# Up-projection of a gated MLP by seven block products instead of eight, with the gated tiles kept in DRAM

## The chip, the cores and the metric

One NeuronCore of a Trainium2 chip runs the whole kernel. The metric is the device time of one execution in microseconds. The engines are called PE (TensorE), DVE (VectorE), ACT (ScalarE), POOL (GpSimd) and SP (SyncE, which issues the DMAs here).

## The reference, cut to what matters

The model is one layer with a mixer sub-layer and a channel sub-layer on 1024 tokens of 1024 channels, all in float32. The change concerns the channel sub-layer:

```python
FFN_DIM = 2816
def conv_ffn(h, w_up, conv_w, conv_b, w_down, rows, cols):
    u, v = jnp.split(h @ w_up, 2, axis=-1)            # (1024, 1024) @ (1024, 2 * 2816)
    u = dwconv2d(u, conv_w, conv_b, rows, cols)       # 3x3, depthwise, on a 16 x 64 grid of tokens
    return (jax.nn.gelu(u) * v) @ w_down
...
        x = x + mx[2] * ox                            # first residual, after w_out of the mixer
        hx2 = modulate(rmsnorm(x, norm_ffn_w[l]), mx[3], mx[4])
        x = x + mx[5] * conv_ffn(hx2, ffn_w_up[l], ffn_conv_w[l], ffn_conv_b[l], ffn_w_down[l], rows, GRID_W)
    return rmsnorm(x, final_norm_w)
```

## The kernel before

Activations lie with channels on the 128 partitions and tokens along the free dimension (T = 1024 tokens, H = 512 in a half). Every matrix product works on float32 numbers split into two parts, `hi` and `lo`, and sums three terms: hi x hi, hi x lo, lo x hi. `gdense` (L117) issues them: for each k tile of 128 input channels three matmuls of 128x128 weights on 512 tokens, for each half. Each matmul has its own weight load. `wload` (L77) loads a tile of weights (128 x 1024, 512 KB) into `raw` and splits it: ACT copies `hi`, DVE subtracts for `lo` (`split`, L164). It does so with high priority, into two rooms used in turn.

The order of the work on each engine is made ahead of the run by the framework's scheduler, from the order of the program, from what is ready by its own estimate, and from priority. On the chip every engine then runs its list in order and waits on semaphores. Generators are interleaved by `weave` (L137): so many steps of a side job for each step of the main one.

`tail` (L1219) holds the channel sub-layer. `wout` (L1112) makes the mixer's output product in two halves of the tokens, with the first residual and the sums of squares for the second norm. `norm` (L1097) sums them over partitions with small matmuls, takes 1/rms, spreads it over the partitions, and its `apply` makes the modulated activations, split into `fh` and `fl` (8 k tiles each, the tiles A0 to A15). The norm of the first half runs beside `wout` of the second half, the norm of the second half beside the first `up`.

`up` (L1127) is run for f = 0 to 21. Tile f of u (weights f) goes into `pu`, a two-bank PSUM tile with tag `d` of which there are two; the convolution runs from there on DVE, eight steps of one tap each after ACT's Identity for the middle tap. Tile f of v (weights 22 + f) goes into two one-bank tiles with tag `s` (four of them). Gelu on ACT, the gating with v on DVE, and the split into `h` and `l` follow, which stay in SBUF (tiles H0 to H15). After f = 6 and f = 13 a round of `down` (L1175) multiplies the seven finished tiles by their part of the down-projection, adding into the residual x1; the last eight tiles are taken by `last_down` (L1191), in three pieces of the tokens, with the final norm beside it. Of the weights of the last round, the first are loaded early into the A tiles, which are free by then.

## Time and profile before

| | us |
|---|---|
| median of 3 runs | 2357.77 (2351.71 to 2358.16) |
| span of the profiled execution | 2358.4 |
| PE busy | 2301.8 (98%) |
| DVE busy | 1617.5 (69%) |
| ACT busy | 1067.5 (45%) |
| POOL busy | 3.4 |

The span runs from the first to the last instruction of one profiled execution. Busy times overlap between engines. The channel sub-layer takes the last 740 us of the span, from 1618.5 us, where `wout` ends, on.

### The profile page before, as it was taken

What the parts mean: (1) busy time and instruction counts of PE and PEld (TensorE: products, weight loads), DVE (VectorE), ACT (ScalarE), POOL (GpSimd) and SP (SyncE); (2) the same over time, 40 slices, a digit from 0 to 9 for tenths busy, and PEclk for the clock granted to TensorE, in tenths of its full rate; (3) what the DMA queues carried; (4) which work ended last, traced back from release to release, by engine and by line L of the source; (5) the groups of instructions that cost most, each with busy time, mean ns of one, the idle gap of its engine ahead of it and who ended that gap; (6) DMA issues with size and microseconds to landing.
All of it is one profiled execution on the core that took longest, in us unless ns stands there. A gap on an engine that the chain in (4) does not pass through costs nothing.

```text
span 2358.4 us, 29544 instructions
## 1 busy us (share of the span) xinstructions
PE 2301.8 (98%) x11530; PEld 1926.7 (82%) x11530; DVE 1617.5 (69%) x2618; ACT 1067.5 (45%) x1633; POOL 3.4 (0%) x16
## 2 busy tenths in 40 slices
PE   7999999999999999999999999999999999999998
PEld 3778878778888888888888878888888888888888
DVE  4877877889978858668876675557765267436655
ACT  4477667677766546646635232333221122112221
POOL 0000000000000000000000000000000000000000
PEclk8999999999999999999999999999999999999999
DMA  6212222144435333423428675532111111111112
GB/s 249 98 60 81 86 83 70 59 128 148 131 100 160 114 119 110 150 83 133 148 92 272 224 240 186 165 100 72 45 53 42 54 49 44 47 53 54 45 54 72
DMA packets 81455, 251.79 MB, mean 107 GB/s; under 512 B 9730, under 2 KB 15906, under 8 KB 76068
## 3 DMA queue, kind: packets, MB, share of 16 engines
q1 hardware_dynamic: 81312, 249.90, 32.5%
q8 instruction: 91, 1.49, 0.3%
q14 instruction: 48, 0.39, 0.1%
q10 hardware_dynamic: 4, 0.01, 0.0%
HBM read 222.33 MB, written 27.54 MB: 106 GB/s over the span
## 4 chain that ended last, share of the span: by engine, by line
PE 78%; DVE 11%; DMA 5%; ACT 4%; issue 2%; DVEq 0%; SPq 0%; ACTq 0%
PE d L124 37%; PE s L124 28%; PE s L982 2%; PE s L990 2%; DMA adar<-in_ada 2%; ACT L L162 2%; PE s L656 2%; DVE wlo L159 1%; DMA gk<-gd 1%; DVE L L159 1%; PE s L931 1%; PE s L932 1%; PE s L314 1%; DVE L L156 1%; DMA raw<-in_w 1%
## 5 line engine op out<-in xcount | busy, mean ns | idle before, releaser
L124 PE MATMUL d<-H,whi 128*128 128x512 f32 x2464 | 690.4, 398 | 1.2 <-ACT whi L162 1.0
L124 PEld LDWEIGHTS d<-H,whi 128*128 128x128 f32 x2464 | 450.6, 188 | 88.7 <-ACT whi L162 1.9
L162 ACT ACTIVATE whi<-raw 128x1024 fp32r<-128x1024 f32 (+1 forms) x194 | 203.2, 1049 | 581.5 <-PE s L124 347.5
L124 PE MATMUL d<-H,wlo 128*128 128x512 f32 x1232 | 385.9, 392 | 0.4 <-DVE wlo L159 0.3
L159 DVE TENSOR_TENSOR wlo<-raw,whi 128x1024 fp32r<-128x1024 f32 (+1 forms) x194 | 234.2, 1209 | 204.3 <-ACT whi L162 201.4
L124 PEld LDWEIGHTS d<-H,wlo 128*128 128x128 f32 x1232 | 230.2, 188 | 49.2 <-DVE wlo L159 1.7
L124 PE MATMUL s<-A,whi 128*128 128x512 f32 x960 | 258.4, 389 | 0.0
L124 PE MATMUL d<-A,whi 128*128 128x512 f32 x960 | 258.3, 389 | 0.0
L124 PE MATMUL s<-H,whi 128*128 128x512 f32 x832 | 251.3, 390 | 0.2 <-ACT whi L162 0.2
L156 DVE SCALAR_TENSOR_TENSOR facc<-d,vec,facc 128x945 f32<-128x945 f32 (+5 forms) x184 | 216.7, 1178 | 11.2 <-ACT facc L162 5.9
L124 PEld LDWEIGHTS d<-A,whi 128*128 128x128 f32 x960 | 180.1, 188 | 37.6
L124 PEld LDWEIGHTS s<-A,whi 128*128 128x128 f32 x960 | 180.2, 188 | 37.3
L124 PEld LDWEIGHTS s<-H,whi 128*128 128x128 f32 x832 | 155.9, 188 | 33.2 <-ACT whi L162 0.7
L162 ACT ACT_TABLE_LOAD x107 | 137.3, 1283 | 76.3 <-DVE cacc L156 28.7
L124 PE MATMUL s<-H,wlo 128*128 128x512 f32 x416 | 157.1, 390 | 2.8 <-DVE wlo L159 2.8
L156 DVE SCALAR_TENSOR_TENSOR M<-s,mods,M 128x512 f32<-128x512 f32 (+1 forms) x72 | 49.6, 690 | 160.7 <-PE s L124 160.5
L124 PE MATMUL d<-A,wlo 128*128 128x512 f32 x480 | 149.2, 389 | 0.2 <-DVE wlo L159 0.2
L124 PE MATMUL s<-A,wlo 128*128 128x512 f32 x480 | 149.1, 389 | 0.0
L124 PEld LDWEIGHTS d<-A,wlo 128*128 128x128 f32 x480 | 90.0, 188 | 19.2 <-DVE wlo L159 0.6
L124 PEld LDWEIGHTS s<-A,wlo 128*128 128x128 f32 x480 | 90.1, 188 | 18.7
L162 ACT ACTIVATE m<-GU,dtt 128x128 f32<-128x128 f32 x256 | 78.9, 389 | 48.5 <-PE s L982 43.5
L156 DVE SCALAR_TENSOR_TENSOR m<-GL,dtt,m 128x128 f32<-128x128 f32 x256 | 77.0, 345 | 29.5 <-ACT m L162 29.0
(274 smaller groups left out, 3191.4 us busy)
## 6 DMA issues: line engine op xcount, KB each, us to landing
raw<-in_w SPq DMA_DIRECT2D x92, 512.0 KB, 3.6
E<-csd SPq DMA_DIRECT2D x32, 1024.0 KB, 4.9
raw<-in_wup SPq DMA_DIRECT2D x44, 512.0 KB, 3.4
R<-csd SPq DMA_DIRECT2D x64, 256.0 KB, 3.9
adar<-in_ada SPq DMA_DIRECT2D x32, 512.0 KB, 4.3
gated<-sg SPq DMA_DIRECT2D x32, 256.0 KB, 2.5
gd<-y SPq DMA_DIRECT2D x32, 256.0 KB, 4.4
gk<-gd SPq DMA_DIRECT2D x32, 256.0 KB, 3.7
```

Source lines behind the costliest of these rows:

```text
L124: nc.tensor.matmul(o, a[:, k, :], b[k][:, xo + s : xo + e], start=(k == 0 and i == 0), stop=(k == kn - 1 and i == 2))
L156: self.nc.vector.scalar_tensor_tensor(out, in0, s, in1, op0=op0, op1=op1)
L159: self.nc.vector.tensor_tensor(out, a, b, op=op)
L162: self.nc.scalar.activation(out, in_, f, **kw)
L314: self.nc.tensor.matmul(ps[:2, :], scc[:, k, :], w[:, k, :], start=(k == 0), stop=(k == 7))
L656: nc.tensor.matmul(pg, a[:, q, :], b[:, s:e], start=(i == 0), stop=(i == 2))
L931: nc.tensor.matmul(ps[:, s - s2, 0, :], btok[:, s, :], xw[:, 0, s, :], start=True, stop=True)
L932: nc.tensor.matmul(ps[:, s - s2, 1, :], btok[:, 7 - s, :], xw[:, 1, 7 - s, :], start=True, stop=True)
L982: nc.tensor.matmul(psy[:, c, :], self.xt[:, c0 + c, h, :], m[:, h, c, :], start=(h == 0), stop=(h == 1))
L990: nc.tensor.matmul(pso[:, c, :], S[:, cc if d == 0 else 7 - cc, d, :], CT[:, cc * P : (cc + 1) * P], start=True, stop=True)
```

## The change

For each f the up-projection is seen as a product of 2 x 2 blocks: two tiles of outputs (u and v) by two halves of the 1024 input channels, times two halves of the channels by two halves of the tokens. Eight block products become seven (`PRODUCTS`), a form of Strassen's with sums of weights (`up_sums`, `up_split`) and sums of activations (`blocks` in `tail`). A block product has 4 k tiles x 3 terms on 512 tokens. Sums and `lo` parts of the weights are made on POOL (`ptt`). Blocks of activations are made once, in `blocks`, for all f. Partial products are collected in PSUM and in three SBUF tiles (`up_product`). Convolution, Gelu and gating of tile f (`up_post`) run beside the products of f + 1. The gated tile is stored to DRAM (`h_d`); `hload` brings it back and splits it for `down`. All 22 `up` come first, then both rounds of `down`, then the last. Two masks of the SSD stage (`mU`, `mL`, two affine_select on POOL) move from `setup` to `ssd`. Comments and docstrings go. Of the diff the part on the channel sub-layer, with deleted lines left out where they are printed above:

```diff
@@ -1124,53 +1124,154 @@
     ROUNDS = [(0, 7), (7, 14), (14, 22)]
-    def up(self, f, x, split, parts):
...
+    PRODUCTS = ("11", "12", "s2", "s1", "s3", "s4", "22")
+    def ptt(self, out, a, b, op):
+        self.nc.gpsimd.tensor_tensor(out, a, b, op=op)
+    def up_load(self, f, x):
+        raw = []
+        for i in range(2):
+            r = self.t(x["pA"], T, f"A{12 + 2 * (f % 2) + i}")
+            self.nc.sync.dma_start(r, self.A["wup"][f + NF * i])
+            raw.append(r)
+        x["raw"][f] = raw
+    def up_sums(self, f, x):
+        u, v = x["raw"][f]
+        q = self.t(self.wp, T, "raw")
+        a, b = q[:, :H], q[:, H:]
+        self.ptt(a, v[:, :H], v[:, H:], ALU.add)
+        self.ptt(b, a, u[:, :H], ALU.subtract)
+        x["sums"][f] = (a, b)
+    def up_split(self, f, p, x):
+        u, v = x["raw"][f]
+        a, b = x["sums"].get(f, (None, None))
+        src = {"11": u[:, :H], "12": u[:, H:], "22": v[:, H:], "s1": a, "s2": b, "s3": a, "s4": b}[p]
+        self.pslot = (self.pslot + 1) % 4
+        w = self.t(self.wp, T, ("whi0", "wlo0", "whi1", "wlo1")[self.pslot], F32R)
+        hi, lo = w[:, :H], w[:, H:]
+        self.act(hi, src, AF.Copy)
+        self.ptt(lo, src, hi.bitcast(F32), ALU.subtract)
+        if p == "s1":
+            self.ptt(a, u[:, :H], v[:, :H], ALU.subtract)
+        elif p == "s2":
+            self.ptt(b, u[:, H:], b, ALU.subtract)
+        x["w"][f, p] = [q.rearrange("p (k m) -> p k m", k=4) for q in (hi, lo)]
+    def up_product(self, f, p, x):
+        st = x["st"].setdefault(f, {})
+        if p == "11":
+            st["u"] = self.t(self.psD, T, "d")
+        elif p == "s3":
+            st["z"] = self.t(self.psS, H, "s")
+        ps = st["z"] if p in ("s3", "22") else st["u"][:, :H] if p == "12" else st["u"][:, H:]
+        hi, lo = x["w"].pop((f, p))
+        for k in range(4):
+            while x["b"][p][k] is None:
+                next(x["blocks"])
+            bh, bl = x["b"][p][k]
+            for i, (a, b) in enumerate(((hi, bh), (hi, bl), (lo, bh))):
+                self.nc.tensor.matmul(ps, a[:, k, :], b, start=(k == 0 and i == 0 and p in ("11", "12", "s3")),
+                                      stop=(k == 3 and i == 2), skip_group_check=True)
+            yield
+        if p == "11":
+            st["s1"] = self.t(self.p1, H, "sql")
+            self.act(st["s1"], ps, AF.Copy)
+        elif p == "12":
+            self.tt(ps, ps, st["s1"], op=ALU.add)
+        elif p == "s2":
+            st["s2"] = self.t(self.p2, H, "ssq")
+            self.act(st["s2"], ps, AF.Copy)
+        elif p == "s1":
+            st["s4"] = self.t(self.p1, H, "s4") if f % 2 else self.t(self.gp, H, "sg")
+            self.act(st["s4"], ps, AF.Copy)
+        elif p == "s3":
+            self.tt(st["s4"], ps, st["s4"], op=ALU.add)
+        elif p == "22":
+            self.tt(st["s2"], ps, st["s2"], op=ALU.add)
+    def up_post(self, f, x):
+        st = x["st"][f]
+        yield
+        acc = self.t(self.p2, T, "facc")
         wc = [self.v("ffn_conv_w", tap * NF + f) for tap in range(9)]
         a3 = acc.rearrange("p (r c) -> p r c", c=64)
...
+        u3 = st["u"].rearrange("p (r c) -> p r c", c=64)
+        self.act(acc, st["u"], AF.Identity, bias=self.v("ffn_conv_b", f), scale=wc[4])
+        for n, tap in enumerate((1, 7, 0, 2, 3, 5, 6, 8)):
+            dy, dx = tap // 3 - 1, tap % 3 - 1
+            r0, r1 = max(0, -dy), 16 - max(0, dy)
+            c0, c1 = max(0, -dx), 64 - max(0, dx)
+            o = a3[:, r0:r1, c0:c1]
+            self.stt(o, u3[:, r0 + dy : r1 + dy, c0 + dx : c1 + dx], wc[tap], o)
+            if n % 2:
+                yield
+        self.act(acc, acc, AF.Gelu_apprx_tanh)
+        yield
+        for i, v in ((1, st["s4"]), (0, st["s2"])):
+            self.tt(acc[:, i * H : i * H + H], acc[:, i * H : i * H + H], v)
+        self.st.dma_start(self.h_d[f], acc)
+        del x["st"][f]
+        yield
+    def ups(self, x):
+        first = [(0, "11"), (1, "11"), (0, "12"), (1, "12"), (0, "s2"), (1, "s2"), (0, "s1"), (1, "s1"), (0, "s4"),
+                 (0, "s3"), (1, "s3"), (1, "s4"), (0, "22")]
+        seq = list(first)
+        for f in range(2, NF):
+            seq += [(f, "11"), (f - 1, "22")] + [(f, p) for p in ("s2", "12", "s1", "s3", "s4")]
+        seq.append((NF - 1, "22"))
+        self.pslot = 0
+        side = []
+        for f in range(2):
+            self.up_load(f, x)
+            self.up_sums(f, x)
+        for q in seq[:2]:
+            self.up_split(*q, x)
+        for i, (f, p) in enumerate(seq):
+            if i + 2 < len(seq):
+                g, q = seq[i + 2]
+                self.up_split(g, q, x)
+                if q == "22" and g + 2 < NF:
+                    self.up_load(g + 2, x)
+            yield from self.up_product(f, p, x)
+            if (f, p) == (1, "s4") or (p == "12" and 1 < f < NF - 1):
+                self.up_sums(f + 1, x)
+            for g in list(side):
+                if next(g, "end") == "end":
+                    side.remove(g)
+            if p == "s4":
+                g = self.up_post(f, x)
+                next(g)
+                side.append(g)
+            if f == NF - 1:
+                for g in {"12": (0, 1), "s1": (2, 3), "s3": (4,), "s4": (5,), "22": (6,)}.get(p, ()):
+                    self.hload(g, x, self.t(x["pA"], T, f"A{12 + g % 4}"))
+        x["side"] = side
+    H_ROOM = (("A0", "A1"), ("A2", "A3"), ("H4", "H5"), ("H6", "H7"), ("A4", "A5"), ("A6", "A7"), ("H0", "H1"),
+              ("H2", "H3"), ("H8", "H9"), ("H10", "H11"), ("H12", "H13"), ("H14", "H15"), ("A8", "A9"), ("A10", "A11"),
+              ("A0", "A1"), ("A2", "A3"), ("H4", "H5"), ("H6", "H7"), ("A4", "A5"), ("A6", "A7"), ("H0", "H1"),
+              ("A14", "A15"))
+    WD_ROOM = (("H2", "H3"), ("H8", "H9"), ("H10", "H11"), ("H12", "H13"), ("H14", "H15"), ("A8", "A9"),
+               ("A10", "A11"), ("A12", "A13"))
+    def room(self, x, tag, dt=F32R):
+        return self.t(x["pA"] if tag[0] == "A" else self.pH, T, tag, dt)
+    def hload(self, f, x, raw=None):
+        raw = self.t(self.p2, T, "facc") if raw is None else raw
+        self.nc.sync.dma_start(raw, self.h_d[f])
+        h, l = [self.room(x, q) for q in self.H_ROOM[f]]
+        self.split(raw, h, l)
         x["h"][f] = (h, l)
...
     def down(self, r, x):
         a, b = self.ROUNDS[r]
@@ -1178,6 +1279,11 @@
         xh, xl = [x["h"][f][0] for f in range(a, b)], [x["h"][f][1] for f in range(a, b)]
         for m in range(8):
             w = self.wload(self.A[f"wd{r}"][m], kn * P, kn)
+            for g in list(x["side"]):
+                if next(g, "end") == "end":
+                    x["side"].remove(g)
+            if a + kn + m < self.ROUNDS[r + 1][1]:
+                self.hload(a + kn + m, x)
             for hf in range(2):
                 s, e = hf * H, hf * H + H
                 ps = self.t(self.psS, H, "s")
@@ -1201,8 +1307,7 @@
             while len(x["wd"]) < min(m + 3, 8):
                 q = len(x["wd"])
                 with (self.prio() if q < 2 else nullcontext()):
-                    hi = self.t(pA, T, f"A{2 * q}", F32R)
-                    lo = self.t(pA, T, f"A{2 * q + 1}", F32R)
+                    hi, lo = [self.room(x, n) for n in self.WD_ROOM[q]]
                     raw = self.t(self.wp, T, "raw")
                     nc.sync.dma_start(raw, self.A[f"wd{r}"][q])
                     self.split(raw, hi, lo)
@@ -1217,22 +1322,83 @@
     WAIT = (5, 3)
     def tail(self, mh, ml, pA, pM, out):
...
         nc, tc = self.nc, self.tc
         with tc.tile_pool(name="t1", bufs=1) as self.p1, tc.tile_pool(name="t2", bufs=2) as self.p2:
             x1 = [self.t(pM, T, f"M{k}") for k in range(8)]
...
+            self.h_d = self.dram([NF, P, T], "hd")
+            x = {"x1": x1, "h": {}, "wd": [], "pA": pA, "raw": {}, "sums": {}, "w": {}, "st": {}}
             sums = {}
...
-            def second(hf):
...
+            halves = lambda q: (q[:, :H], q[:, H:])
+            first = [halves(self.t(pA, T, f"A{k}", F32R)) for k in range(8)]
+            x["b"] = {p: [None] * 4 for p in self.PRODUCTS}
+            x["b"]["11"], x["b"]["12"] = first[:4], first[4:]
+            b8, b9 = [self.t(pA, T, f"A{k}") for k in (8, 9)]
+            b11 = [b8[:, :H], b8[:, H:], b9[:, :H], self.t(self.p1, H, "s4")]
+            def shifted(k, s, e, rs, t):
+                self.stt(t, x1[k][:, s:e], self.sc2[:, k : k + 1], rs, op0=ALU.mult, op1=ALU.mult)
+                return self.mods[:, 24 + k : 25 + k]
+            def apply0(k, rs):
+                t = self.t(self.p2, T, "facc")[:, :H]
+                xh, xl = first[k]
+                shift = shifted(k, 0, H, rs, t)
+                self.act(xh, t, AF.Identity, bias=shift)
+                if k < 4:
+                    self.act(b11[k], t, AF.Identity, bias=shift)
+                self.stt(xl, t, shift, xh.bitcast(F32), op0=ALU.add, op1=ALU.subtract)
+            def blocks():
+                for _ in range(3):
+                    yield
+                r = self.token_rs(self.p1, sums[1], H, 1.0 / D, "fr")
+                for _ in range(3):
+                    yield
+                rs = self.t(self.psS, H, "s")
+                self.spread(self.p2, r, rs, "fr")
+                yield
+                def split(p, k, src, tag):
+                    q = halves(self.room(x, tag))
+                    self.act(q[0], src, AF.Copy)
+                    self.tt(q[1], src, q[0].bitcast(F32), op=ALU.subtract)
+                    x["b"][p][k] = q
+                    return q
+                both, t2 = [], []
+                for k in range(4):
+                    q = halves(self.t(self.pH, T, f"H{12 + k}"))
+                    both.append(q)
+                    for i in range(2):
+                        shift = shifted(k + 4 * i, H, T, rs, q[i])
+                        self.act(q[i], q[i], AF.Identity, bias=shift)
+                    a, b = halves(self.t(self.p2, T, "facc"))
+                    self.tt(a, q[1], q[0], op=ALU.subtract)
+                    self.tt(b, a, b11[k], op=ALU.add)
+                    t2.append(split("s2", k, b, f"H{4 + k}"))
+                    yield
+                for k in range(4):
+                    a, _ = halves(self.t(self.p2, T, "facc"))
+                    self.ptt(a, both[k][0], b11[k], ALU.subtract)
+                    split("s1", k, a, f"H{k}")
+                    yield
+                for k in range(4):
+                    split("s4", k, both[k][1], f"A{(10, 11, 8, 9)[k]}")
+                    yield
+                for k in range(4):
+                    a, _ = halves(self.t(self.p2, T, "facc"))
+                    self.tt(a, both[k][1], both[k][0], op=ALU.subtract)
+                    split("s3", k, a, f"H{8 + k}")
+                    yield
+                for k in range(4):
+                    a, _ = halves(self.t(self.p2, T, "facc"))
+                    b21 = first[4 + k]
+                    self.tt(a, b21[0].bitcast(F32), t2[k][0].bitcast(F32), op=ALU.subtract)
+                    self.tt(a, a, b21[1].bitcast(F32), op=ALU.add)
+                    self.tt(a, a, t2[k][1].bitcast(F32), op=ALU.subtract)
+                    split("22", k, a, f"H{12 + k}")
+                    yield
             def final(i):
                 s, e = self.PIECES[i]
@@ -1245,16 +1411,13 @@
             for m in range(8):
                 nc.sync.dma_start(x1[m], self.A["xT"][m])
+            self.weave(self.wout(mh, ml, x1, 0, sums), None, 1)
+            self.weave(self.wout(mh, ml, x1, 1, sums), self.norm(sums[0], H, apply0, (5, 3)), self.RATIO[4])
+            x["blocks"] = blocks()
+            self.weave(self.ups(x), x["blocks"], self.RATIO[4])
+            for r in range(len(self.ROUNDS) - 1):
+                self.down(r, x)
             side = None
...
-            ends = {b: r for r, (a, b) in enumerate(self.ROUNDS[:-1])}
...
-                self.weave(self.up(f, x, f == 0, 2 if f == NF - 1 else 1), side, self.RATIO[4])
...
-                    self.down(ends[f], x)
             for i in range(len(self.PIECES)):
                 self.weave(self.last_down(i, x, sums), side, self.RATIO[5])
                 side = final(i)
```

## Rows read from the trace of the kernel before

**Rows 1.** The page: span, and busy time, share and instructions of each engine.
```profile
span 2358.4 us, 29544 instructions
PE 2301.8 (98%) x11530; PEld 1926.7 (82%) x11530; DVE 1617.5 (69%) x2618; ACT 1067.5 (45%) x1633; POOL 3.4 (0%) x16
```
**Rows 2.** The chain that ended last, in time: start us, us, what (L124 is `gdense`).
```profile
1618.48 4.08 PE d L124 x18
...
1643.24 10.88 PE d L124 x48
...
1784.68 87.04 PE s L124 x384
...
2241.64 56.55 PE s L124 x258
```
**Rows 3.** Waits of PE, 1520 to 2358 us: total us, times, longest.
```profile
PE d L208 <- DVE frdg L207: 1.9, 1, 1.9
PE d L198 <- DVE sql L159: 0.9, 1, 0.9
```
**Rows 4.** Stretches: us; busy (count) PE PEld DVE ACT POOL; granted PEclk; DMA, GB/s.
```profile
1665.00:1686.76 21.76, 21.76 (x97) 18.02 (x97) 17.95 (x17) 5.34 (x6) 0.00 (x0) 1.00 0.16 48
1784.68:1860.84 76.16, 76.16 (x337) 63.06 (x337) 30.60 (x32) 10.45 (x11) 0.00 (x0) 1.00 0.16 50
```
**Rows 5.** Groups by shape, 1618 to 2300 us: busy us, mean ns, idle before.
```profile
L156 DVE SCALAR_TENSOR_TENSOR facc<-d,vec,facc 128x945 f32<-128x945 f32 x84 | 101.0, 1202 | 2.9
L159 DVE TENSOR_TENSOR wlo<-raw,whi 128x1024 fp32r<-128x1024 f32 x43 | 52.5, 1221 | 103.4 <-ACT whi L162 102.9
L159 DVE TENSOR_TENSOR facc<-facc,s 128x512 f32<-128x512 f32 x44 | 28.3, 684 | 4.0 <-ACT facc L162 3.1
L162 ACT ACTIVATE facc<-d,vec 128x1024 f32<-128x1024 f32 x21 | 25.0, 1192 | 0.0
L162 ACT ACTIVATE facc<-facc 128x1024 f32<-128x1024 f32 x21 | 22.3, 1064 | 13.0 <-DVE facc L156 13.0
L162 ACT ACTIVATE sg<-M 128x512 f32<-128x512 f32 x6 | 3.8, 630 | 21.4 <-DVE M L156 21.4
L162 ACT ACTIVATE facc<-d,vec 128x512 f32<-128x512 f32 x2 | 1.5, 770 | 6.3 <-PE d L124 6.3
```
**Rows 6.** Groups of POOL by shape, the whole run.
```profile
L707 POOL MEMSET xt<- 128x512 f32 x2 | 1.0, 532 | 349.3 <-PE d L124 349.3
...
L282 POOL TENSOR_SCALAR_AFFINE_SELECT mU<-ones 128x128 f32<-128x128 f32 x1 | 0.3, 292 | 0.0
...
L240 POOL MEMSET btok<- 64x4 f32 x1 | 0.1, 100 | 0.1
```
**Rows 7.** DMA issues: count, KB each, median us from issue to landing.
```profile
raw<-in_wup SPq DMA_DIRECT2D x44, 512.0 KB, 3.4
...
M<-ad SPq DMA_DIRECT2D x8, 512.0 KB, 6.0
```
**Rows 8.** Second norm, second half, PE and DVE: start us, us, what [idle before].
```profile
1622.40 0.28 PE L198 MATMUL d<-ones,ssq 128*128 128x1 f32 x2
...
1627.79 1.41 DVE L156 SCALAR_TENSOR_TENSOR facc<-M,sc,d 128x512 f32<-128x512 f32 x2 [0.58 <-PE d L208]
1629.33 1.41 DVE L156 SCALAR_TENSOR_TENSOR A<-facc,mods,A 128x512 fp32r<-128x512 f32 x2
1630.66 1.40 DVE L156 SCALAR_TENSOR_TENSOR facc<-M,sc,d 128x512 f32<-128x512 f32 x2
```
**Rows 9.** Stretches at the start of the run (columns as in rows 4).
```profile
20.00:25.00 5.00, 0.98 (x4) 0.92 (x4) 3.77 (x8) 3.60 (x5) 0.00 (x0) 0.57 1.01 414
25.00:30.00 5.00, 0.80 (x4) 0.83 (x4) 4.83 (x9) 2.81 (x3) 0.00 (x0) 0.50 0.67 274
...
35.00:40.00 5.00, 4.03 (x17) 3.57 (x18) 2.45 (x11) 0.84 (x2) 0.00 (x0) 0.50 0.00 0
40.00:45.00 5.00, 5.00 (x23) 2.09 (x22) 1.57 (x4) 2.62 (x4) 0.00 (x0) 0.88 0.25 84
```

More of the change, by code (lines that the diff above doesn't have):

```diff
@@ L276, in setup @@
         self.ones = self.t(cpool, P, "ones")
-        self.mU = self.t(cpool, P, "mU")
-        self.mL = self.t(cpool, P, "mL")
         nc.gpsimd.memset(self.ones, 1.0)
@@ L702, in ssd @@
             self.bc, self.grp, self.pair, self.E, self.yst = {}, {}, {}, {}, {}
+            self.mU = self.t(q1, P, "mU")
+            self.mL = self.t(q1, P, "mL")
+            nc.gpsimd.affine_select(out=self.mU, in_=self.ones, pattern=[[1, P]], compare_op=ALU.is_ge,
+                                    fill=0.0, base=0, channel_multiplier=-1)
+            nc.gpsimd.affine_select(out=self.mL, in_=self.ones, pattern=[[-1, P]], compare_op=ALU.is_ge,
+                                    fill=0.0, base=0, channel_multiplier=1)
             dtt, cst, wtt = [self.t(q1, [NC, 16, 4], n) for n in ("dtt", "cst", "wtt")]
@@ L1125 @@
     ROUNDS = [(0, 7), (7, 14), (14, 22)]
-    def up(self, f, x, split, parts):
-        A, p2, fh, fl = self.A, self.p2, x["fh"], x["fl"]
-        pu = self.t(self.psD, T, "d")
-        spans = [[(0, H)], [(H, T)]] if split else [self.FULL]
-        wu = self.wload(A["wup"][f])
-        if split:
-            wv = self.wload(A["wup"][NF + f])
-            pv = [self.t(self.psS, H, "s") for _ in range(2)]
-            for sp in spans[:1]:
-                yield from self.gdense(pu, wu, fh, fl, sp)
-                yield from self.gdense(pv, wv, fh, fl, sp)
-            spans = spans[1:]
-        for sp in spans:
-            yield from self.gdense(pu, wu, fh, fl, sp)
-        acc = self.t(p2, T, "facc")
+    PRODUCTS = ("11", "12", "s2", "s1", "s3", "s4", "22")
@@ L1142, in up @@
+    def up_post(self, f, x):
+        st = x["st"][f]
+        yield
+        acc = self.t(self.p2, T, "facc")
         wc = [self.v("ffn_conv_w", tap * NF + f) for tap in range(9)]
         a3 = acc.rearrange("p (r c) -> p r c", c=64)
-        u3 = pu.rearrange("p (r c) -> p r c", c=64)
-        step = 16 // parts
-        for q in range(parts):
-            lo, hi = q * step, q * step + step
-            self.act(a3[:, lo:hi], u3[:, lo:hi], AF.Identity, bias=self.v("ffn_conv_b", f), scale=wc[4])
-            for tap in (1, 7, 0, 2, 3, 5, 6, 8):
-                dy, dx = tap // 3 - 1, tap % 3 - 1
-                r0, r1 = max(lo, -dy), min(hi, 16 - max(0, dy))
-                c0, c1 = max(0, -dx), 64 - max(0, dx)
-                o = a3[:, r0:r1, c0:c1]
-                self.stt(o, u3[:, r0 + dy : r1 + dy, c0 + dx : c1 + dx], wc[tap], o)
@@ L1155, in up @@
-        if not split:
-            wv = self.wload(A["wup"][NF + f])
-            pv = [self.t(self.psS, H, "s") for _ in range(2)]
-        for sp in spans:
-            yield from self.gdense(pv, wv, fh, fl, sp)
-        i = f % 8
-        h = self.t(self.pH, T, f"H{2 * i}", F32R)
-        l = self.t(self.pH, T, f"H{2 * i + 1}", F32R)
-        step = T // parts
-        for q in range(parts):
-            sl = slice(q * step, q * step + step)
-            self.act(acc[:, sl], acc[:, sl], AF.Gelu_apprx_tanh)
-            for i in range(2 * q // parts, 2 * (q + 1) // parts):
-                hs = slice(i * H, i * H + H)
-                self.tt(acc[:, hs], acc[:, hs], pv[i])
-            self.act(h[:, sl], acc[:, sl], AF.Copy)
-            self.tt(l[:, sl], acc[:, sl], h[:, sl].bitcast(F32), op=ALU.subtract)
+        u3 = st["u"].rearrange("p (r c) -> p r c", c=64)
@@ L1247, in tail @@
                 nc.sync.dma_start(x1[m], self.A["xT"][m])
-            side = None
-            for hf in range(2):
-                self.weave(self.wout(mh, ml, x1, hf, sums), side, self.RATIO[4])
-                side = second(hf)
-            ends = {b: r for r, (a, b) in enumerate(self.ROUNDS[:-1])}
-            for f in range(NF):
-                self.weave(self.up(f, x, f == 0, 2 if f == NF - 1 else 1), side, self.RATIO[4])
-                side = None
-                if f in ends:
-                    self.down(ends[f], x)
+            self.weave(self.wout(mh, ml, x1, 0, sums), None, 1)
[4 more added lines that the diff above has]
+                self.down(r, x)
+            side = None
             for i in range(len(self.PIECES)):
```

13 lines of the change are left out of this document (removed).

## The prediction, made before the change was run

> **What bounds the kernel now.** I read the page first: TensorE (PE) is busy 98% of the 2358.4 us span, VectorE (DVE) 69%, ScalarE (ACT) 45%, GpSimd (POOL) nothing [rows 1]. A share is a mean over stages, so next comes the chain that ended last, for the stretch from the end of w_out (1618.5 us) on. It is PE line 124 throughout: 48 matmuls in 10.88 us for each half of an `up`, and 384 in 87.04 us for the last half `up` before a round together with that round [rows 2]. Both are 0.2267 us a matmul, so PE runs without a gap. The waits of PE from 1520 us to the end confirm it: two, 2.8 us together, both in the second norm [rows 3]. One `up` in steady state takes 21.76 us, PE busy for all of it at full clock, DVE 17.95, ACT 5.34, POOL 0 [rows 4]. So a matmul removed here is worth 0.2267 us, as long as the other engines keep up, and PE never waits for new data.
>
> **Part 1, the products.** An `up` has 2 tiles x 8 k x 3 terms x 2 halves = 96 matmuls. Seven products of 4 k x 3 terms on 512 tokens are 84, of the same shape. Seen as time: 96 x 0.2267 = 21.76 us (as the row says) becomes 19.04 us; 22 times the 2.72 us saved is **59.8 us**. The two rounds of `down` and the last one keep their matmuls.
>
> **Part 2, what each tile asks of the other engines in 19.04 us.** DVE: eight taps at about 1.20 us (9.6), three half-wide additions of products at 0.68 (2.0), two gatings at 0.68 (1.4): 13.0 us, less than now, since the splits of weights and of h leave it [rows 5]. ACT: seven half-wide copies at 0.63 (4.4), three evictions of PSUM at 0.77 (2.3), one Identity of 1.19 and one Gelu of 1.06: 9.0 us [rows 5]. Both fit. POOL is new: seven `lo` subtractions and four sums a tile, 11 operations of 128x512 with two inputs. No row shows one. From below: a memset of 128x512, which reads nothing, 0.53 us. An affine_select of 128x128, one input, takes 0.29; less the 0.10 of a memset of four columns, that is 1.5 ns a column [rows 6]. A second input doubles this at most: 0.10 + 512 x 3.0 ns = 1.64 us. I take 1.21 (memset's 0.84 ns a column plus 0.66 ns for each input), nearest to the affine_select, which reads. Then 11 take 13.3 us, between 5.8 and 18.0: inside 19.04 even at the upper end. So in steady state I charge nothing; the cover is POOL's spare 5.7 us a tile, and if POOL took over 1.73 us an operation, PE would follow POOL. A gain is excluded, as PE has no wait there now.
>
> The Trainium skill (GPSIMD Engine Reference, Performance versus the Vector engine) gives 4497 ns for a tensor_tensor of 2048 columns; a quarter of it, an estimate of 1.12 us an operation, would make 12.4 us a tile and the same sum. No run here shows it yet.
>
> Three new waits of PE lie in each tile: products 11, s2 and s1 add into the same half of the `d` tile, and each is copied out by ACT before the next adds to it. One other product of 2.72 us stands between each pair; a copy needs 0.77 [rows 5]. One Gelu or Identity ahead of it on ACT still fits (1.19 + 0.77), two and a wait do not: see rival B. The store of h waits on SP for the gating; behind it stand only the loads of the tile after next, some 15 us early at 3.4 us each [rows 7]: nothing.
>
> **Part 3, the head (where I expect the loss).** Let 0 be the end of w_out, 1618.5 us in the old trace. Only products 11 and 12 of tiles 0 and 1 can run on the first half of the tokens: 4 x 2.72 = 10.9 us. All else needs blocks of the second half. Today the sums for the norm are issued at 1622.40 and the first scaling starts at 1627.79, 5.4 us later; with the change they are issued after three steps (2.0 us), so scaling starts at about 7.4 [rows 8]. From there DVE must do, half-wide: 20 operations for the s2 blocks (two scalings, two sums, one `lo` for each k), 4 for s1, 4 for s4, 8 for s3, 16 for 22, and four additions of products: 56 at the 0.66 us at which such operations follow each other [rows 8], 37.0 us, and 0.6 for one unhidden ACT step: until 45. The taps of tile 0 come after them in the program, 9.6 us: until **54.6**. Tile 2 can't begin before, since `d` has two rooms and tiles 0 and 1 hold both. Thirteen products stand ahead of tile 2: 13 x 2.72 = 35.4 us. PE so loses **19 us**: some 7 before the s2 products, the rest ahead of tile 2. From below: if the taps are scheduled ahead of the 22 blocks (10.6 us of DVE), the loss is 9.
>
> The clock: early in the run PE was nearly idle for some 10 us, the granted clock went to 0.50 (1.2 GHz), stayed there while PE was again 80% busy, and came back in the slice at 40 us [rows 9]. A stall of 10 us before tile 2 may cost the same: 10 us at half clock are 5 us. I take 4, ends 0 and 10.
>
> POOL and DVE side by side: no row shows both on SBUF at once. From below nothing. From above every POOL operation of the head (nine `lo`, ten sums, about 19 x 1.21 = 23 us) holds DVE. Of DVE's 56 operations 44 have both inputs in SBUF (29 us). If these and POOL's excluded each other, 29 + 23 = 52 us would have to fit into the 47 us of the head: at least **5 us** more. I take that 5; ends 0 and 23. The Trainium skill (SBUF — State Buffer, Who interferes with whom) says that a DVE instruction with two SBUF inputs and a GpSimd instruction that reads SBUF wait for one another in full, and that one with a PSUM input does not; by the rule the steady taps (PSUM and SBUF) stay free, by none of it the sum would be 5 us better.
>
> Against this stands what the head costs today: from 1618.48 to the end of the last `up` (2241.64 + 10.88 = 2252.52) are 634.04 us, and the work is 22 x 21.76 + 2 x 76.16 = 631.04 [rows 2]. So **3.0 us** are lost now, and are within the 19.
>
> **Part 4, from the last tile to the first round.** Seven h tiles come back from DRAM (6.0 us for a load of that size at worst [rows 7]), and each needs 1.06 of ACT and 1.22 of DVE [rows 5] within the last tile's products. DVE then has 13.0 + 7 x 1.22 = 21.5 us for 19.04, and the last tile's own first taps (2.4) stand ahead of h6: about 5 us late, of which the first half product of `down` hides little, since it needs all seven. A weight pair of `down` may also wait for the last product (1.06 + 1.22). I charge **5**, ends 1 and 9. The other 15 come in the rounds, where DVE has much room (30 us in 76 [rows 4]): nothing. Moving the two masks to the SSD stage costs two POOL operations of 0.29 us [rows 6] ahead of their first use: nothing.
>
> **Sum** against the profiled 2358.4 us, whose span is all there is and 0.6 over the median of 2357.8: -59.8 - 3.0 + 19 + 4 + 5 + 5 = -29.8: 2328.6, against the median **2328**. The ends of the single costs give 2306 (9, 0, 0, 1) to 2357 (19, 10, 23, 9).
>
> **Rivals.** *A, POOL sets the pace (slower).* If POOL held off DVE's taps too, or its operation cost over about 1.85 us, a tile would take longer than 19.04 + 30/22 = 20.4 us and the gain is gone. Its price in the first case: 13.0 + 13.3 = 26.3 us a tile, 22 x 7.3 = 160 more: about 2490. For it: POOL does nothing today, so no row tests it. Against: the upper bound of 1.64 still fits, and the taps read PSUM. 0.12.
> *B, ACT's order holds PE up.* ACT runs in order. Its 21 Gelus wait today for the taps, 13.0 us in all [rows 5], and PE doesn't feel it [rows 3]; with the change an eviction may stand behind one. One eviction late by 1.4 us in each tile is 22 x 1.4 = 31 us: 2359, no change. For it: slack of one product only. Against: 9.0 us of ACT in 19.04. 0.16.
> *C, the head is nearly free.* The scheduler fills it with other products: below 2306. Against: nothing else is ready. 0.04.
> That the matmuls are not fewer can't be: the loop shows it.
>
> **Numbers.** Forecast 0.68 (2306 to 2357, centre 2328), A 0.12, B 0.16 (2340 to 2375), C 0.04. Faster or slower by under 0.3% (7 us) can't be told from no change. Faster: 0.62 of the forecast, C, and 0.06 of B: 0.72. Same: 0.06 and 0.05 of B: 0.11. Slower: A and 0.05 of B: 0.17. The range leaves out A, C and the top of B: 2306 to 2370.
>
> **What would show it.** Right: a steady tile of 19.04 us with PE gapless, POOL near 70% busy there, idle PE ahead of products s2 and of tile 2, and about 5 us ahead of the first round. Wrong: PE waiting for `lo` from POOL in every tile (A), for ACT's copies (B), or a POOL operation over 1.7 us.

## The result: slower by 3.3%, and the profile after

| | before | after |
|---|---|---|
| median, us | 2357.4 (2351.71 to 2358.16, 4 runs) | 2433.02 (2429.6 to 2435.15, 4 runs) |
| span of the profiled execution, us | 2358.4 | 2431.4 |

The ratio is 1.033 (95% interval 1.0312 to 1.0343), where 2328 (2306 to 2370) was forecast. The page of after, first its busy times (compare [rows 1]); PE does 264 matmuls less, as Part 1 counted (22 x 12), and is idle far longer:

```profile
span 2431.4 us, 29821 instructions
PE 2295.0 (94%) x11266; PEld 1896.6 (78%) x11266; DVE 1645.0 (68%) x2667; ACT 1155.0 (48%) x1830; POOL 328.1 (13%) x262
```

The places are found by three times on PE: the end of w_out (1613.10 us), the first product of tile 2 (1692.56) and the first matmul of the rounds (2173.16). The first stretch, the **head**, takes 79.5 us. It holds 14 products, not the 13 of the program: the scheduler put product (1, 22), which stands behind the first product of tile 2, ahead of it (168 matmuls come before 1692.56). The second stretch so holds 140 products, and 480.6 / 140 x 7 = **24.03 us for each seven**; the rest takes 258.2 us, PE without a gap at its start, as the chain of waits shows (compare [rows 2]):

```profile
2173.16 198.29 PE s L124 x882
```

The stretch between the head and the rounds, PE's waits in it (total us, times, longest; the 7.1 us for `facc` are those that end the head) and 50 us of it (columns as in [rows 4], where a tile of before stands):

```profile
PE s L1179 <- ACT whi L162: 19.5, 10, 2.9
PE s L1179 <- ACT wlo L162: 18.9, 10, 2.8
PE d L1179 <- DVE facc L156: 7.1, 1, 7.1
PE s L1179 <- POOL whi L1131: 6.7, 10, 1.2
PE s L1179 <- POOL wlo L1131: 6.1, 10, 0.6
```
```profile
1900.00:1950.00 50.00, 45.01 (x182) 35.33 (x181) 27.60 (x28) 15.57 (x25) 28.87 (x23) 0.93 0.20 66
```

Before, PE waited for no weights here at all [rows 3]. Now it stops in every tile, always at an `s` product, first for its hi and then for its lo part. POOL, whose results are late, is busy for only 58% of the time. So it isn't short of time; its list must be looked at. POOL's instructions in one tile (start us, us, what, idle before and by whom), and PE's of the same stretch:

```profile
1902.74 1.30 POOL L1131 TENSOR_TENSOR raw<-A,raw 128x512 f32<-128x512 f32 x1
1904.28 1.29 POOL L1131 TENSOR_TENSOR whi<-A,whi 128x512 fp32r<-128x512 f32 x1 [0.24 <-ACT whi L162]
1909.37 1.30 POOL L1131 TENSOR_TENSOR raw<-A 128x512 f32<-128x512 f32 x1 [3.80 <-DMA A<-in_wup]
1910.62 1.30 POOL L1131 TENSOR_TENSOR whi<-A,whi 128x512 fp32r<-128x512 f32 x1
1911.88 1.30 POOL L1131 TENSOR_TENSOR raw<-raw,A 128x512 f32<-128x512 f32 x1
1913.14 1.28 POOL L1131 TENSOR_TENSOR wlo<-raw,wlo 128x512 fp32r<-128x512 f32 x1
1914.49 1.26 POOL L1131 TENSOR_TENSOR raw<-A,A 128x512 f32<-128x512 f32 x1
1916.50 1.28 POOL L1131 TENSOR_TENSOR whi<-raw,whi 128x512 fp32r<-128x512 f32 x1 [0.74 <-ACT whi L162]
```
```profile
1910.90 2.88 PE L1179 MATMUL d<-H,wlo 128*128 128x512 f32 x12
1916.47 0.83 PE L1179 MATMUL s<-H,whi 128*128 128x512 f32 x2 [2.69 <-ACT whi L162]
1917.83 1.22 PE L1179 MATMUL s<-H,whi 128*128 128x512 f32 x2 [0.52 <-POOL whi L1131]
1918.85 5.21 PE L1179 MATMUL d<-A,whi 128*128 128x512 f32 x12
```

`raw<-A` is the first sum of the **next** tile. It waits 3.80 us for that tile's weights to arrive, and behind it stand the lo part of product 12 (`whi<-A`), that of s1 (`wlo<-raw`), the difference from which s3 is made (`raw<-A,A`) and the lo part of s3 (`whi<-raw`, the last line). PE's list has four matmuls of s3 ahead of product 12, so PE stands until POOL has come that far. The program writes the two sums behind the lo part of s3; the scheduler that makes each engine's list moved them ahead of the lo part of s1: in 13 of 18 tiles one ahead of the lo part of 12 and one behind it, as here, in the other 5 both right behind it. After the stop the granted clock is lower: the twelve matmuls of product 12 take 5.21 us (granted 0.52 from 1918.8 to 1924 us, close to the lower level of 1.2 GHz), where twelve took 2.88 before it (granted 1.00 from 1908 to 1916 us).

### The profile page after: what moved, and what is told of

The parts are those of the page before. It is cut to its first block, busy times and chain, and to the rows that moved or that the text cites. A ratio compares the mean times of both kernels' runs of the same rounds, so it can differ in the third digit from the quotient of the medians.

```text
span 2431.4 us, 29821 instructions
## 1 busy us (share of the span) xinstructions
PE 2295.0 (94%) x11266; PEld 1896.6 (78%) x11266; DVE 1645.0 (68%) x2667; ACT 1155.0 (48%) x1830; POOL 328.1 (13%) x262
## 4 chain that ended last, share of the span: by engine, by line
PE 68%; DVE 12%; POOL 6%; issue 5%; DMA 5%; ACT 3%; DVEq 0%; SPq 0%; POOLq 0%; ACTq 0%
PE d L124 29%; PE s L124 17%; PE d L1179 7%; POOL raw L1131 3%; PE s L1179 2%; PE s L982 2%; PE s L990 2%; DMA adar<-in_ada 2%; PE s L650 2%; POOL wlo L1131 2%; POOL whi L1131 2%; DVE wlo L159 1%; DVE L L159 1%; DMA gk<-gd 1%; PE s L931 1%
## 5 line engine op out<-in xcount | busy, mean ns | idle before, releaser
L124 PE MATMUL d<-H,whi 128*128 128x512 f32 x2464 | 691.0, 398 | 0.5 <-ACT whi L162 0.3
L124 PEld LDWEIGHTS d<-H,whi 128*128 128x128 f32 x2464 | 451.2, 189 | 88.1 <-ACT whi L162 1.0
L124 PE MATMUL d<-H,wlo 128*128 128x512 f32 x1232 | 386.4, 393 | 1.0 <-DVE wlo L159 1.0
L162 ACT ACTIVATE whi<-raw 128x1024 fp32r<-128x1024 f32 (+2 forms) x194 | 183.8, 949 | 274.7 <-PE s L124 106.6
L124 PEld LDWEIGHTS d<-H,wlo 128*128 128x128 f32 x1232 | 230.2, 188 | 50.1 <-DVE wlo L159 2.5
L156 DVE SCALAR_TENSOR_TENSOR facc<-d,vec,facc 128x945 f32<-128x945 f32 (+2 forms) x176 | 214.1, 1220 | 72.0 <-ACT facc L162 68.2
L159 DVE TENSOR_TENSOR wlo<-raw,whi 128x1024 fp32r<-128x1024 f32 (+1 forms) x150 | 180.8, 1207 | 89.4 <-ACT whi L162 88.3
L124 PE MATMUL s<-H,whi 128*128 128x512 f32 x640 | 192.2, 390 | 0.5 <-ACT whi L162 0.5
L124 PEld LDWEIGHTS s<-H,whi 128*128 128x128 f32 x640 | 119.8, 188 | 26.1 <-ACT whi L162 0.9
L124 PE MATMUL s<-A,whi 128*128 128x512 f32 x448 | 127.4, 389 | 1.1 <-ACT whi L162 1.1
L124 PE MATMUL s<-H,wlo 128*128 128x512 f32 x320 | 119.7, 391 | 2.8 <-DVE wlo L159 2.8
L1179 PE MATMUL d<-A,whi 128*128 128x512 f32 x396 | 113.0, 434 | 7.1 <-DVE facc L156 7.1
L1179 PE MATMUL d<-A,wlo 128*128 128x512 f32 x396 | 112.5, 433 | 4.3 <-POOL wlo L1131 1.5
L1179 PEld LDWEIGHTS d<-A,whi 128*128 128x128 f32 x396 | 84.2, 216 | 29.1 <-issue 7.5
L1179 PE MATMUL s<-H,wlo 128*128 128x512 f32 x264 | 75.8, 420 | 28.4 <-ACT wlo L162 18.9
L124 PEld LDWEIGHTS s<-A,whi 128*128 128x128 f32 x448 | 84.0, 188 | 19.0 <-ACT whi L162 1.5
```

Of the source, the lines that this page charges most:

```text
L124: nc.tensor.matmul(o, a[:, k, :], b[k][:, xo + s : xo + e], start=(k == 0 and i == 0), stop=(k == kn - 1 and i == 2))
L156: self.nc.vector.scalar_tensor_tensor(out, in0, s, in1, op0=op0, op1=op1)
L159: self.nc.vector.tensor_tensor(out, a, b, op=op)
L162: self.nc.scalar.activation(out, in_, f, **kw)
L1179: self.nc.tensor.matmul(ps, a[:, k, :], b, start=(k == 0 and i == 0 and p in ("11", "12", "s3")), stop=(k == 3 and i == 2), skip_group_che ...
```

## The experiments

All times in one table. "Head" and "seven" are measured as above, in the profiled execution, with 140 products in the second stretch; in e1 and e3, where PE keeps the order of the program, 141, and in e9 141 and a half. The kernel before, beside each group, had 2353 (e1 to e4), 2359 (e5 to e8), 2358 (e9 and later). But for e6, e9 and e10 each time is that of one execution; those of the kernel before went from 2349 to 2362, so a few us of time say little, and the stretches are read from the traces.

| kernel | head, us | seven products, us | time, us |
|---|---|---|---|
| after | 79.5 | 24.03 | 2433.0 |
| e1, PE's order fixed | 79.5 | 21.38 | 2383.7 |
| e2, POOL's order fixed | 77.4 | 20.07 | 2352.4 |
| e3, both fixed | 77.5 | 21.41 | 2387.0 |
| e4, POOL's work on DVE | 67.1 | 20.40 | 2351.5 |
| e5, no late loads | 82.1 | 20.13 | 2360.9 |
| e6, e2 with the head on DVE | 68.3 | 20.15 | 2348.7 |
| e7, e2 with no POOL in the head | 61.7 | 20.09 | 2342.7 |
| e8, e6 without the 22 blocks | 60.6 | 20.20 | 2340.1 |
| e9, e6 with taps before 22 | 59.0 | 20.30 | 2345.1 |
| e10, e2 again | 77.5 | 20.12 | 2355.1 |
| e11, e2 with the sums early | 79.0 | 24.43 | 2441.7 |
| e12, e11 without late loads | 77.5 | 22.53 | 2399.9 |

**The order of the lists: e1, e2, e3.** In e2 every POOL operation of `ptt` keeps the order of the program; in e1 the first matmul of a product stands behind the last one of the product before; e3 has both.

```
-        self.nc.gpsimd.tensor_tensor(out, a, b, op=op)
+        self.tc.keep_in_program_order(self.nc.gpsimd.tensor_tensor(out, a, b, op=op))    # e2, e3
...
+                if k == 0 and i == 0 and x.get("last") is not None:
+                    self.behind(q, x["last"])                                             # e1, e3
```

> One edge of order per product keeps TensorE's products in the order of the program; in the changed kernel's trace the first matmuls of s3 stand ahead of the whole of product 12, and TensorE waits there for a lo part from GpSimd in every tile. Nothing else differs. Theory O (the order of the lists costs the time, TensorE's own order above all): a steady tile falls from 24.0 us to about 21.5, 20 tiles, so about 2380. Theory P (GpSimd's chain of subtractions and sums is too long for a tile, whatever the order): the tile stays at 24.0 and the time at 2431. If only GpSimd's own order counts, it stays as well.

> One edge of order per operation keeps GpSimd in the order of the program; in the changed kernel's trace the two sums of the next tile stand ahead of the lo parts of 12, s1 and s3, and wait for weights from DRAM (33.6 us in 14 waits). TensorE's order is left to the scheduler. Theory O: GpSimd no longer stands still while the lo parts wait, the tile falls by about 2 us and the time to about 2390; if TensorE's own order counts more, to 2410 only. Theory P: 2431. Theory W (the weights come too late because their rooms come free too late): 2431 as well, since the sums still wait for them.

> Both edges of the two kernels before together. Theory O: a steady tile of 19.0 to 20 us, TensorE without gaps, so 20 tiles x 4 to 5 us less than 2431: about 2340. The head (79 us from the end of w_out to the first matmul of tile 2) stays. Theory P: still above 22 us a tile, 2400 or more. Theory W: waits for weights remain visible on GpSimd or ScalarE and the tile stays near 23 us.

In e2 the loss between the products is nearly gone: PE is busy 99% of the same 50 us at full clock, and POOL 70%.

```profile
1900.00:1950.00 50.00, 49.52 (x216) 39.81 (x215) 30.49 (x33) 20.50 (x31) 35.21 (x28) 1.00 0.25 83
```

The gain is more than theory O's 2 us a tile. PE's own order helps less, as the text on e1 expected (21.4 us, 2384), and brings waits of its own. PE's waits in e1, 1600 us to the end, then POOL's list in one of its tiles:

```profile
PE d L1183 <- DVE d L159: 19.6, 21, 2.4
PE d L1183 <- ACT ssq L162: 14.6, 21, 0.9
```
```profile
1908.73 1.30 POOL L1131 TENSOR_TENSOR raw<-A 128x512 f32<-128x512 f32 x1 [0.27 <-DMA A<-in_wup]
1910.10 1.30 POOL L1131 TENSOR_TENSOR raw<-raw,A 128x512 f32<-128x512 f32 x1
1911.36 1.30 POOL L1131 TENSOR_TENSOR wlo<-A,wlo 128x512 fp32r<-128x512 f32 x1
```

With the products in a strict order 12 follows s2 and s1 follows 12 directly, and each waits 0.7 to 0.9 us until ACT's copy or DVE's sum after the product before it is done; in e2 matmuls of s3 stand between, four and then seven or eight. That is also why e3 missed its 19 to 20 us: it has e1's waits.

So the harm took both lists. In e1 POOL has both sums ahead of the lo part of 12 in every tile, as shown, and yet PE waits for no weights from tile 2 to the last product: there s3, whose lo part POOL makes after those of 12 and s1, has its place behind them on PE too. Where PE is left to the scheduler, four matmuls of s3 stand ahead of 12, in after as in e2; then POOL's order decides between 24.03 and 20.07 us, while with PE's order fixed it decides nothing (21.38 and 21.41). Even in e2 these four are not free, as their third, the first to need the lo part, waits for POOL in each tile:

```profile
1937.36 0.73 PE L1179 MATMUL s<-H,wlo 128*128 128x512 f32 x2 [0.36 <-POOL wlo L1131]
```

**Without POOL: e4.** `ptt` works on DVE (`nc.vector` for `nc.gpsimd`).

> All operations that the change gives to GpSimd run on VectorE instead, in the same places of the program. VectorE then has 13.0 + 11 x 0.66 = 20.3 us of work a tile, above 19.04. Theory P: VectorE's operation is half as long as GpSimd's (0.66 against 1.29 us), the chain gets shorter, so a tile of 20.5 to 22 us and a time of 2360 to 2390. Theory O: the order is made anew by the scheduler and may invert again; VectorE's taps now stand ahead of lo parts, so no better than 2400. The head gets longer by the 20 operations that move there, about 13 us, less what GpSimd and VectorE cost each other there now.

Seven products take 20.40 us with DVE busy for 94% of 1900 to 1950 us; the time, 2351, is below the range of theory P, and the head is 12 us shorter than in after, not longer. Without POOL's list the steady loss is gone; the head's has a second cause, to which e6 to e9 go.

**Place, or late load: e5, e11, e12.** e5 leaves out the weight loads from tile 2 on.

> The changed kernel, but the up weights are loaded only for tiles 0 and 1 and used again for the other twenty tiles (their loads are left out, so the output is not the reference's). GpSimd's list keeps its order: the sums of tile f+1 stand ahead of four or five lo parts of tile f. Theory W (the harm comes from that order only because the sums wait at the head of the list for a load that lands late, 33.6 us in 14 waits): without the load nothing waits there, GpSimd needs 14.2 us of work for a tile of 19.0, and a steady tile falls from 24.0 us to 19.3 to 20.0; the time falls from 2433 to 2345 to 2365. Rival Q (the order alone is enough, since the sums of f+1 put 4 x 1.3 = 5.2 us of work in front of lo parts that TensorE needs sooner): a steady tile stays at 22 us or more and the time at 2395 or more. Between the two the shares can be read off.

The loss went, as theory W said, but the run doesn't show why: without loads the scheduler put the sums behind the lo part of s4, so the list had changed with them. e11 therefore fixes POOL's order as in e2, with both sums ahead of the lo part of 12 (in the changed kernel one of them or both stand right behind it), and e12 takes the loads away from that:

```
-            if (f, p) == (1, "s4") or (p == "12" and 1 < f < NF - 1):
+            if (f, p) == (1, "s4") or (p == "11" and 1 < f < NF - 1):      # e11, e12
                 self.up_sums(f + 1, x)
...
+        if f >= 2:                                                          # e5, e12, in up_load
+            x["raw"][f] = x["raw"][f % 2]
+            return
```

> The kernel of e2 with one thing moved: GpSimd, still in a fixed order, makes the sums of tile f+1 before the lo part of product 12 of tile f, as its list stood in the changed kernel, instead of behind the lo part of s3. Everything else is as in e2. Theory O (this place in GpSimd's list is what costs the time): TensorE's waits on ScalarE's hi and GpSimd's lo parts come back, seven steady products take 23 to 24.5 us instead of 19.9, and the time is 2415 to 2440. Rival R (what e2 mended was something else that the fixed order brought, such as the order of the lo parts among themselves or TensorE's list): seven products stay at 19.6 to 20.5 us, and the time at 2350 to 2365.

> The kernel of e11 without the weight loads from tile 2 on (the weights of tiles 0 and 1 are used again, so the output is not the reference's): the same fixed order on GpSimd, but nothing to wait for at the sums. In e5 GpSimd's list had changed with the loads, so this run tells the two apart. Theory W (the place harms only because the sums wait there for a late load): seven steady products take 19.6 to 20.5 us and the time is 2350 to 2362. Rival Q (2.6 us of sums ahead of the lo parts are enough by themselves): seven products take 22 us or more and the time is 2395 or more.

e11 has the whole loss again by that one move. POOL's wait for loads and PE's waits in it, tile 2 to the rounds; then PE's in e12 (POOL has no such wait there):

```profile
POOL raw L1131 <- DMA A<-in_wup: 22.5, 18, 1.9
PE s L1179 <- ACT wlo L162: 23.1, 10, 3.1
PE s L1179 <- ACT whi L162: 21.9, 10, 2.9
```
```profile
PE s L1182 <- ACT wlo L162: 11.4, 10, 1.6
PE s L1182 <- ACT whi L162: 10.8, 10, 1.6
```

Theory W fell in e12: without any load to wait for, seven products still take 22.53 us. Of the 4.4 us that e11 loses on e2 for each seven, 24.43 - 22.53 = **1.9 are the late load, and 22.53 - 20.07 = 2.5 are the place alone**, about the two sums themselves (2 x 1.30 us). Both hold what the lower clock behind each stop costs (granted 0.91 in e11, 0.94 in e12 and 1.00 in e2, from 1900 to 1950 us). Work that nobody needs yet, put into an in-order list ahead of work that PE stands waiting for, here cost about its own length in each tile, though POOL is idle elsewhere in the tile; in e1, where PE doesn't stand waiting for it, the same place cost nothing (the load is hardly late there either: POOL waits 0.7 us for it in all).

**The head: e6 to e9.** e6 is e2 with the POOL operations of tiles 0 and 1 and of the s1 blocks on DVE. e7 makes copies on ScalarE of them. e8 is e6 without building the blocks of product 22. e9 is e6 with product (0, 22) behind (2, 11) and the 22 blocks built behind the taps of tile 0.

```
+        if self.head:                                 # tiles 0 and 1; the s1 blocks likewise
+            self.tt(out, a, b, op=op)                 # e6, e8, e9;  e7: self.act(out, a, AF.Copy)
+        else:
+            self.tc.keep_in_program_order(self.nc.gpsimd.tensor_tensor(out, a, b, op=op))
...
+                x["b"]["22"] = x["b"]["s3"]           # e8, in place of the loop that builds them
...
-                 (0, "s3"), (1, "s3"), (1, "s4"), (0, "22")]
+                 (0, "s3"), (1, "s3"), (1, "s4")]     # e9; (0, "22") follows (2, "11")
```

> The kernel of e2 (GpSimd in program order), but the operations on GpSimd of the head (sums and lo parts of tiles 0 and 1 and the four differences for the blocks of s1) are on VectorE; from tile 2 on GpSimd works as in e2. Theory X (in the head GpSimd and VectorE take turns where a VectorE operation has both inputs in SBUF, so each GpSimd operation of 1.29 us takes VectorE more than the 0.6 us it costs there): the head, from the end of the output projection to the first product of tile 2, falls from 77.4 us to about 67 as in e4, the steady tile stays at 19.3, and the time falls from 2352 to about 2342. Rival V (VectorE's own list is what is full, and GpSimd's share costs it nothing): 24 more operations by 0.6 us make the head longer, 85 to 92 us, and the time 2360 or more.

> The kernel of e2, but those same operations of the head are replaced by copies of the first input on ScalarE (so the output is not the reference's): VectorE has exactly its work of e2 and GpSimd none until tile 2. Theory X: VectorE's operations with both inputs in SBUF take 0.68 us again instead of 0.9 to 1.8, the head falls from 77.4 us to 52 to 60, the time to 2327 to 2337. Rival V (VectorE's volume, and the order of its list, set the head): 72 to 78 us, time 2347 to 2353. Rival S (ScalarE, with 24 copies by 0.63 us more, becomes the bound): ScalarE is busy over 90% of the head and TensorE's waits name it; the head is 65 us or more.

> The kernel of e6, but the four blocks for the seventh product are not built (the blocks of s3 are used in their place, so the output is not the reference's): 16 operations of VectorE and 4 of ScalarE less in the head. Theory D (VectorE is busy without a break from the scaling to the taps of tile 0, so the head is as long as its list): the head falls by 16 x 0.62 = 10 us, from 67 to about 57, the time by as much. Rival P (TensorE's order and the waits for lo parts set the head, and VectorE has slack): it falls by less than 4 us.

> The kernel of e6, but the seventh product of tile 0 stands behind the first product of tile 2, and the blocks of the seventh product are built after the taps of tile 0 instead of before them (the same operations in another order). Theory D (VectorE's list is full from the scaling on, and the first product of tile 2 waits 6.1 us for the last tap of tile 0, which stands behind the 16 operations of those blocks): the first product of tile 2 begins 58 to 62 us after the end of the output projection instead of 68.3, and where TensorE then waits for the blocks it waits less than it saved, so the time falls from 2349 to 2338 to 2345. Rival G (the blocks now come late for the seventh products, and the wait only changes its place): the first product of tile 2 begins as early, but TensorE stops 5 us or more at the seventh products, and the time stays at 2346 to 2352.

e7's head is 15.7 us shorter than e2's, with the same work on DVE; 61.7 is just over the 52 to 60 of theory X, far from V's 72 and below the 65 of S (ACT is busy for 68% of that head). The groups of DVE in the head (busy us, mean ns), first e2, then e7:

```profile
L159 DVE TENSOR_TENSOR H<-facc,H 128x512 fp32r<-128x512 f32 x16 | 16.8, 1063 | 2.3 <-ACT H L162 1.8
L159 DVE TENSOR_TENSOR facc<-H 128x512 f32<-128x512 f32 x8 | 8.6, 1091 | 0.0
L156 DVE SCALAR_TENSOR_TENSOR facc<-d,vec,facc 128x945 f32<-128x945 f32 x6 | 6.9, 1184 | 0.0
L156 DVE SCALAR_TENSOR_TENSOR H<-M,sc,s 128x512 f32<-128x512 f32 x8 | 5.7, 742 | 0.6 <-PE s L208 0.6
```
```profile
L159 DVE TENSOR_TENSOR H<-facc,H 128x512 fp32r<-128x512 f32 x16 | 11.5, 732 | 0.9 <-ACT H L162 0.8
L156 DVE SCALAR_TENSOR_TENSOR facc<-d,vec,facc 128x945 f32<-128x945 f32 x6 | 6.9, 1195 | 0.0
L156 DVE SCALAR_TENSOR_TENSOR H<-M,sc,s 128x512 f32<-128x512 f32 x8 | 5.7, 743 | 0.6 <-PE s L208 0.6
L159 DVE TENSOR_TENSOR facc<-H 128x512 f32<-128x512 f32 x8 | 5.4, 688 | 0.1
```

Beside POOL the operations of the two groups with both inputs in SBUF take 1.06 to 1.09 us on average instead of 0.69 to 0.73; taps and scalings, with one input in PSUM (`d`, `s`), take the same in both. The two groups grow by 8.5 us. Two more, `A<-H,A` and `facc<-A,H` (four each), go from 0.69 to 1.2 us, 4.1 us more; other operations with two inputs in SBUF (`facc<-facc,A`, 0.68 in both runs) show no difference, so not every one is held up. In e6 DVE does the work itself at 0.69 us an operation, and the head is 9.1 us shorter than in e2. The moved work costs DVE less than POOL's did from beside it.

e8 takes 16 more operations from DVE (9.9 us at 0.62) and 7.7 us off the head: DVE's volume does set it. e9 does all the work, in another order, and tile 2 begins 9.3 us sooner than in e6. What then? PE's waits from there on, e9:

```profile
PE d L1184 <- ACT ssq L162: 3.1, 1, 3.1
PE s L1184 <- POOL whi L1134: 2.3, 4, 1.2
PE s L1184 <- ACT H L162: 1.3, 1, 1.3
```

From the end of w_out to the first round e9 takes 469.3 us and e6 471.3: 2.0 of the 9.3 us are kept. A product and a half (4.1), which e6 makes ahead of that point (14 products, here 12 and a half), had only been moved behind it. Rival G was nearer, though the waits that took the rest are spread (3.1 for `ssq`, 1.3 for a block), not one of 5 us at product 22.

**Against the kernel before: e10, e6, e9.**

> The kernel of e2 once more, in five rounds, for an interval. With its one look (2352 beside 2353 for the kernel before): ratio to the kernel before 0.996 to 1.001, so that the seven products with GpSimd in program order, and nothing else changed, give back the 76 to 80 us that the changed kernel loses. A rival would have that look by chance, and the ratio over 1.005.

e10: ratio 0.9988 (0.9976 to 1.0), so seven products in POOL's fixed order are worth next to nothing. e6: 0.9959 (0.9946 to 0.9972), and e9: 0.9953 (0.9936 to 0.9969) are 0.4 to 0.5% faster than the kernel before, and, by the ratios to it, 3.6% faster than the change as it was made (0.9959 / 1.0328 and 0.9953 / 1.0328).

## Why the prediction was wrong, point by point

What bounds the kernel, and **Part 1**, held: PE, 264 matmuls less. **Part 4** was of the right size. Right ahead of the first round PE waits only 1.1 us, but 2.6 more in the last tile (0.2, 1.2 and 1.2 us, one of them for a copy on ACT that stands behind the split of an h tile); in e2 the last seven products and the wait take 23.9 us, 4.8 more than 19.04, where 5 were charged.

**Part 2 is the step that failed**: "in steady state I charge nothing; the cover is POOL's spare 5.7 us a tile". The sizes under it were right: 11 operations, 1.29 us each (1.21 taken), 14.2 us a tile, POOL at 70% in e2, as forecast. The estimate of 1.12 us from the Trainium skill (GPSIMD Engine Reference, Performance versus the Vector engine) is 13% below the measured 1.29. But spare time over a tile says nothing of when in the tile a result is there. I weighed POOL's throughput, and in rival A also whether it holds off the taps; it was 58% busy, and a tap still takes 1.2 us. I asked of each DMA only whether its queue was free, not which waiting instruction it would put at the head of POOL's list. I took the products to run in the order of the program, too, where s3 stands behind s1. From the first product of tile 2 to the first round the forecast is 140 x 2.72 + 4 + 5 = 389.8 us (the 141st ran in the head); after takes 480.6, e2 401.3. These are the two stretches (columns as in [rows 4]), first after, then e2:

```profile
1692.56:2173.15 480.59, 426.19 (x1680) 332.13 (x1680) 267.29 (x268) 162.72 (x247) 274.55 (x212) 0.93 0.22 72
1691.04:2092.38 401.34, 392.07 (x1680) 312.37 (x1680) 267.88 (x268) 164.94 (x247) 276.88 (x214) 1.00 0.26 86
```

So 79.3 of the 90.8 us too many go with POOL's order: PE's waits at `s` are 51 us (5 in e2), and the same 1680 matmuls take 34 us more of PE's time (426.2 against 392.1), at a granted clock of 0.93 against 1.00. The other 11.5 are in e2 too, and are the smaller cost that I also put at nothing: between the first seven products and the last, seven take 19.54 to 19.87 us there, not 19.04, and 0.4 to 0.65 us of that lie in each tile at the third matmul of s3, which waits for its lo part.

**Part 3 had the mechanism and missed sizes.** 54.6 + 5 us were forecast for the head, 79.5 measured. Of the exclusion I took 5, the least that would not fit; e2 against e7 gives 15.7, since DVE is full (e8) and can't make up for operations that are stretched, and since POOL does more there than I counted: 28 operations and 42.7 us in e2's head, some of them for tile 2, where I had about 19 and 23 us. The rule of the Trainium skill (SBUF — State Buffer, Who interferes with whom) agrees with the trace in both halves, two SBUF inputs (0.69 against 1.09 us) and an input in PSUM (1.19 against 1.18). Without POOL, e7's 61.7 us are 7.1 above the 54.6: scaling starts 9.4 us after the end of w_out instead of 7.4, and twelve taps stand on DVE ahead of tile 2, not eight, as those of tile 1 are mixed in (4 x 1.17 = 4.7). That the clock falls behind the stall is right, though not the 4 us: the first product of tile 2 takes 5.46 us in after instead of 2.88, and in e2 the first seven take 24.1 us, 4.5 more than later ones, 2.2 of it waits, so that about 2.3 are left for the clock. The rounds are as forecast: 2358.4 - 1618.5 - 29.8 = 710.1 us from w_out's end on, less 59.6 and 392.5, leaves 258.0, and 258.2 were measured.

**Rival B** stayed away (one wait of 0.7 us for `sql`, one of 1.2 for `s` in the last tile); in e1 copies hold PE up, but with no Gelu ahead of them. **Rival C** was wrong. Of what should show the prediction wrong, "PE waiting for `lo` from POOL in every tile" was named, and came; I had tied it to the wrong condition.

## What to carry to other kernels

When work goes to an idle engine, the question isn't only whether it has time, but in which order it will do it: write down its list for one period with the moment at which each input is there and each result is needed. What waits for a transfer, or is only needed in the next period, belongs behind the results that the bounding engine waits for. If a scheduler makes the lists, look at them in the trace and force the order where it is wrong: on the helper, as in e2, which was the better here, or on the bounding engine, as in e1. And a saving on the bounding engine is only worth what the start-up leaves of it: here the matmuls save 59.8 us, and the head takes most of it even in e2, where 14 products worth 38.1 us take 77.4.

## What the runs showed of the hardware that I had not expected

The cost of POOL beside a full DVE: on DVE an operation of 128x512 with two SBUF inputs takes 0.69 us, on POOL 1.29; in the head of e2 POOL's own take 1.4 to 1.95 us and stretch DVE's to 1.06 and more. Even an operation of four columns was held up beside POOL; in e2's head:

```profile
L186 DVE TENSOR_SCALAR fra<-fra 128x4 f32<-128x4 f32 x1 | 1.1, 1147 | 0.0
```

In e4, without POOL, the same one took 0.17 us. What of the stretch falls on which of POOL's operations wasn't tried.
